# A hybrid decoder layer on one core: keys in natural order in one tile, 144-column scores for the first block, one convolution tap by ScalarE, and a rearranged end

## The chip, the core and the metric

The kernel runs on one core of a Trainium2 chip. Its engines work at the same time, each through a list of instructions of its own: TensorE (PE: matrix products, PEld is its loading of the stationary operand), VectorE (DVE), ScalarE (ACT), GpSimd (POOL) and SyncE (SP, which here only issues transfers). Matrix products land in PSUM banks; everything else lives in SBUF. Transfers go through 16 DMA engines. The metric is the time of one execution on the device, in microseconds (us): the median of several runs.

## The reference, cut to what matters

A sequence of 1,024 rows of 1,024 features gets 16 learned meta rows in front (1,040 positions, all in float32). One layer is computed: a combined input projection feeds an attention group (8 heads of 64 features, 2 key heads, window of 128, one sink per head) and a recurrent group (causal convolution of width 4, gated linear recurrence), then come an output projection and a feed-forward part.

```python
h = concat([meta, x])
u = rmsnorm(h, g_pre_mix)
q, k, v, xr, yr = split(u @ w_in)         # 512, 128, 128, 512, 512 columns
# attention: position i sees keys i-127 .. i, none before the meta rows
s = where(valid, q @ k.T * 64**-0.5, -1e30)
m = max(s.max(-1), sink)
p = exp(s - m) / (exp(s - m).sum(-1) + exp(sink - m))
attn = p @ v
# recurrent group
xr = causal_depthwise_conv(xr, conv_w, conv_b)   # 4 taps and a bias
hr = rg_lru(xr, w_a, b_a, w_x, b_x, lam)
mix = concat([attn, gelu(yr) * hr]) @ w_out
h = h + rmsnorm(mix, g_post_mix)
f = square(relu(rmsnorm(h, g_pre_ffn) @ w_ff1)) @ w_ff2
out = (h + rmsnorm(f, g_post_ffn))[16:]
```

## The kernel before, in words

**Precision.** Every operand of a matrix product is split into a high part in the format fp32r and a low part that holds the rest. ScalarE makes the high part (L96 in `split`, L117 where a scale comes in), VectorE the low part (L99, L118). `mm3` then issues three matmuls (L125 high by high, L128 high by low, L129 low by high) into one PSUM bank. For the scores two matmuls do (L596 with the keys' high part, L600 with the low one): the query tile holds high in 64 of its partitions and low in the other 64, and the key tiles hold the same key twice, once in each half of the partitions. `mirror_k` makes that second copy by transfers that SP issues.

**Stages.** Up to about 58 us the input rows are normalised, transposed and projected to the keys, the values, the first query pair and the first convolution input. From there to about 185 us comes the attention, woven with the remaining projections. Then follow the gates and the recurrence, the output projection (up to about 330 us), and the feed-forward part, which takes two thirds of the time: both its products run as seven block products instead of eight.

**Attention.** The 8 heads are 4 pairs (`j`), the 1,024 positions 8 blocks of 128 in two halves. `scores(j, half, q)` makes the scores of four blocks of a head pair, two blocks to a tile `sn` (tag "c", four slices of 257 columns: 2 heads x 2 blocks). For each block TensorE multiplies the queries with the keys of the block before and of the block itself, 256 columns. Block 0 has only the 16 meta keys before it. In the kernel before these stand in a tile of their own, `km`, at the end of 112 zero columns; its scores come as two groups of 128 columns, 4 matmuls instead of 2, and a second mask (`mask1`) excludes the zero columns. VectorE then adds the mask and takes the row's minimum of the negated scores in one instruction (L616), ScalarE takes the exponential and its sum over 257 columns, the sink being the last (L82). VectorE forms the reciprocal (L628), GpSimd adds the two halves of 128 columns, which hold no common position (L632), VectorE scales by the reciprocal (L633). `attend` runs one step later: TensorE transposes (L644), the result is split (L96, L99), GpSimd separates the two halves again by selects (L648, four for two blocks), TensorE multiplies with the values (L658), and ScalarE and VectorE put the two halves of the product together (L671, L672).

**Fills.** Between these steps `next_fill` puts one projection each: queries of pairs 1 to 3, convolution inputs 1 to 3, the four gates `y`. A query projection ends in L117 (ScalarE) and L118 (VectorE, two of them for each bank), which empty its PSUM bank "acc". A convolution input ends in `sink_x`, a ScalarE copy (L460) in four pieces. Where `y` is given to `new_x`, in this kernel for convolution 2 alone, ScalarE also computes the first tap with the bias from the same bank (L462). `conv` otherwise starts with that tap by VectorE (L682, 1,040 columns), and then adds three taps by VectorE (L687).

**The end.** The last block product is finished by row tile (`finish_late`, tiles `j` = 0 to 3). Tiles 0 to 2 have one part of 512 columns, tile 3 two parts of 256 columns (`HALVES`) in two banks, whose last product's three `q` steps run last. Each part's result is added to the accumulator (first `combine`), ScalarE squares it and sums (L1371), `gffn_b` scales it (second `combine`; both record L1022); then come a square root, its reciprocal (L1416), two output instructions per tile (L1418) and two transfers of 256 KB (L1421). The outputs of a tile are `held`: they may run only behind the next tile's first sum.

**What sets the order.** Each engine's list is made by the scheduler of the framework, which goes by priority (the order in which the code is written, with `deferred` work later), by data, and by the number of buffers of each tag: "b" 17, "c" 8, "d" 4, "e" 2, "ws" 4, "raw" 2, and 2 banks each of "acc", "s", "pt" and "o" in PSUM. Where the code says `behind(name, ins)`, `ins` is to stand behind the instruction `name` of its engine. Tile names in what follows are such a tag and a running number.

## Time and profile before

| | us |
|---|---|
| median of 3 runs | 955.39 (954.9 to 955.9) |
| the profiled execution | 955.25 |
| its span, first instruction to last | 953.5 |
| TensorE busy | 942.0 (99%) |
| VectorE busy | 682.4 (72%) |
| ScalarE busy | 498.3 (52%) |
| GpSimd busy | 152.7 (16%) |
| share of TensorE in the chain that ended last | 88% |

Busy times are those of the profiled execution. In the rows that follow, a row of the chain or of the instructions in order has its start in the span, its duration, the engine, and the operation with what it writes and reads (`out<-in`, numbers left out) or the line. A row of a stretch has the stretch, then the busy time summed over its instructions for TensorE, its weight loads, VectorE, ScalarE and GpSimd, the granted TensorE clock (1.00 is full), the busy share of the DMA engines, and GB/s. A row of a group has the number of its instructions (x), their busy time and the mean duration of one in nanoseconds, or the shortest, the median and the longest.

### The profile page before, as it was taken

To read this page: it belongs to the slowest core of one execution; us is meant where nothing else is said; L and a number is where in the kernel's file an instruction comes from. 1 tells how busy PE (TensorE), PEld (TensorE's weight loads), DVE (VectorE), ACT (ScalarE), POOL (GpSimd) and SP (SyncE) were. 2 spreads that over 40 slices of the span, in tenths; PEclk is the share of its full clock that TensorE was granted. 3 is DMA by queue.
4 is the path that set the end of the run, shared out by engine and by line. 5 is a ranking of instruction groups with operands and counts; after the bars stand their busy time and mean duration, and the time that the engine had idled before them with its cause. 6 is when DMAs were issued, how large, how long until landed. Compare 5 with 4: busy or idle time off the path is not lost.

```text
span 953.5 us, 12448 instructions
## 1 busy us (share of the span) xinstructions
PE 942.0 (99%) x4677; PEld 785.7 (82%) x4677; DVE 682.4 (72%) x968; ACT 498.3 (52%) x822; POOL 152.7 (16%) x196
## 2 busy tenths in 40 slices
...
GB/s 293 49 56 34 45 2 34 67 17 117 42 166 192 153 181 238 158 284 177 218 160 216 157 177 217 226 153 109 171 179 188 208 218 185 185 190 155 116 84 89
DMA packets 85629, 140.76 MB, mean 148 GB/s; under 512 B 5785, under 2 KB 48937, under 8 KB 85569
## 3 DMA queue, kind: packets, MB, share of 16 engines
...
q14 instruction: 24, 0.19, 0.1%
...
## 4 chain that ended last, share of the span: by engine, by line
PE 88%; DVE 7%; ACT 2%; issue 1%; DMA 1%; POOL 1%; DVEq 0%; SPq 0%; ACTq 0%; POOLq 0%
PE ps_acc L125 10%; PE ps_acc L128 10%; PE ps_acc L129 10%; PE ps_pt L128 6%; PE ps_pt L129 6%; PE ps_pt L125 6%; PE ps_s L125 6%; PE ps_s L129 6%; PE ps_s L128 6%; PE ps_o L125 5%; PE ps_o L128 5%; PE ps_o L129 5%; DVE c L852 1%; PE ps_o L658 1%; PE ps_o L996 1%
## 5 line engine op out<-in xcount | busy, mean ns | idle before, releaser
L96 ACT CAST ws<-raw 128x1024 fp32r<-128x1024 f32 (+1 forms) x70 | 71.8, 1025 | 118.9 <-PE ps_o L128 45.8
L99 DVE TENSOR_TENSOR ws<-raw,ws 128x1024 fp32r<-128x1024 f32 (+1 forms) x71 | 85.4, 1203 | 45.5 <-ACT ws L96 45.5
L125 PE MATMUL ps_acc<-a,ws 128*128 128x256 f32 (+2 forms) x256 | 85.5, 334 | 1.1 <-ACT d L460 1.0
L129 PE MATMUL ps_acc<-a,ws 128*128 128x256 f32 (+2 forms) x256 | 85.0, 333 | 0.0
L128 PE MATMUL ps_acc<-a,ws 128*128 128x256 f32 (+2 forms) x256 | 85.0, 332 | 0.0
L99 DVE TENSOR_TENSOR b<-b,b 128x1024 fp32r<-128x1024 f32 (+2 forms) x48 | 57.6, 1199 | 25.5 <-PE ps_o L128 19.8
L96 ACT CAST ws<-e 128x1024 fp32r<-128x1024 f32 x42 | 44.0, 1047 | 57.0 <-PE ps_o L128 31.4
L96 ACT CAST b<-b 128x1024 fp32r<-128x1024 f32 (+2 forms) x48 | 49.5, 1030 | 38.8 <-DVE b L1022 36.4
L99 DVE TENSOR_TENSOR ws<-e,ws 128x1024 fp32r<-128x1024 f32 x42 | 51.3, 1222 | 20.0 <-ACT ws L96 20.0
L648 POOL TENSOR_SCALAR_AFFINE_SELECT c<-c 128x512 fp32r<-128x512 f32 x64 | 55.8, 893 | 26.8 <-ACT c L96 20.6
L125 PEld LDWEIGHTS ps_acc<-a,ws 128*128 128x128 f32 x256 | 48.2, 188 | 6.4 <-ACT d L460 1.2
L129 PEld LDWEIGHTS ps_acc<-a,ws 128*128 128x128 f32 x256 | 48.2, 188 | 5.1 <-issue 0.2
L178 POOL TENSOR_TENSOR rs<-ms,half_pow 128x1 f32<-128x1 f32 x26 | 19.3, 749 | 205.9 <-DVE ms L174 204.7
L128 PEld LDWEIGHTS ps_acc<-a,ws 128*128 128x128 f32 x256 | 48.1, 188 | 4.6 <-issue 0.4
L125 PE MATMUL ps_acc<-ws,b 128*128 128x512 f32 (+1 forms) x120 | 46.3, 385 | 0.0
L129 PE MATMUL ps_acc<-ws,b 128*128 128x512 f32 (+1 forms) x120 | 46.2, 385 | 0.0
L128 PE MATMUL ps_acc<-ws,b 128*128 128x512 f32 (+1 forms) x120 | 46.1, 384 | 0.0
L125 PE MATMUL ps_pt<-ws,b 128*128 128x512 f32 x112 | 44.2, 394 | 0.0
L128 PE MATMUL ps_pt<-ws,b 128*128 128x512 f32 x112 | 44.1, 393 | 0.0
L129 PE MATMUL ps_pt<-ws,b 128*128 128x512 f32 x112 | 43.9, 392 | 0.0
L125 PE MATMUL ps_s<-ws,b 128*128 128x512 f32 x110 | 43.4, 395 | 0.0
L129 PE MATMUL ps_s<-ws,b 128*128 128x512 f32 x110 | 43.2, 393 | 0.0
...
## 6 DMA issues: line engine op xcount, KB each, us to landing
raw<-in_w_ff_dram SPq DMA_DIRECT2D x58, 512.0 KB, 4.4
e<-in_w_ff_dram SPq DMA_DIRECT2D x42, 512.0 KB, 4.1
raw<-in_w_in_dram SPq DMA_DIRECT2D x12, 512.0 KB, 5.1
d<-in_w_ff_dram SPq DMA_DIRECT2D x12, 512.0 KB, 4.2
s_dram<-d POOLq DMA_DIRECT2D x12, 512.0 KB, 4.4
e<-in_w_ff_dram POOLq DMA_DIRECT2D x10, 512.0 KB, 5.8
raw<-in_w_ff_dram POOLq DMA_DIRECT2D x10, 512.0 KB, 5.8
c<-in_x_dram SPq DMA_DIRECT2D x8, 512.0 KB, 8.9
```

What stands on the lines that cost most here:

```text
L96: nc.scalar.copy(hi, src)
L99: low = nc.vector.tensor_tensor(lo, src, f32(hi), op=ALU.subtract).ins
L125: ins = nc.tensor.matmul(dst, lh, rh, start=start, stop=False, skip_group_check=True).ins
L128: nc.tensor.matmul(dst, lh, rl, start=False, stop=False, skip_group_check=True)
L129: last_mm[0] = nc.tensor.matmul(dst, ll, rh, start=False, stop=stop, skip_group_check=True).ins.name
L178: last_pow[0] = nc.gpsimd.tensor_tensor(rs[:n], ms[:n], half_pow[:n], op=ALU.pow).ins.name
L648: nc.gpsimd.affine_select(out=m[:, :, side, :], in_=f32(m)[:, :, 1, :], pattern=[[0, 4], [-sign, P]], compare_op=op, fill=0.0, base=0, cha ...
L658: nc.tensor.matmul(po[:, :, oc : oc + n], v, m[:, :, pc : pc + n], start=first and k == 0, stop=last and k == 1, skip_group_check=True,)
L852: return nc.vector.tensor_tensor_scan(r, a, gi, 0.0, op0=ALU.mult, op1=ALU.add).ins
L996: nc.tensor.transpose(pt[:, i, :], xn[:, kc * P : (kc + 1) * P], ident)
```

## The change

*Keys.* The high and low key tiles (`khh`, `kl`) get 1,040 columns in natural order, the meta keys first. `km` and `mask1` go. Block 0's scores are one group of 144 columns (16 meta keys and 128 of its own), 2 matmuls instead of 4 for each head; L616 and L82 run over 144 and 145 columns there, and GpSimd sets the 112 columns that are now not written to zero, once for each head pair. `sink_k` loses the special case of the meta keys, and the mirror transfers go from 512 to 528 columns for the first half (512 for the second), without the two for `km`.

*Convolution 1.* `new_x` gives `y` for channel group 1 too: its first tap and bias come from ScalarE, in four pieces, and its L682 goes.

*The end.* `finish_late` no longer puts the held outputs of the tile before behind the first sum together. In tile 3, with two parts, one held output is released behind the scaling of each part. Tile 3's own outputs are three, of 512, 256 and 256 columns, issued by SP, ScalarE and SP, instead of two of 512.

The diff, cut:

```diff
@@ -284,13 +284,12 @@
-    khh = [slot("b", [P, T], F32R) for _ in range(2)]
-    kl = [slot("b", [P, T], F32R) for _ in range(2)]
+    khh = [slot("b", [P, TT], F32R) for _ in range(2)]
+    kl = [slot("b", [P, TT], F32R) for _ in range(2)]
     HALF = (slice(0, HD), slice(HD, P))
-    km = const.tile([P, 2, 2, P], F32R, name="km")
     vm = const.tile([P, 2, P], F32R, name="vm")
-    nc.gpsimd.memset(f32(km), 0.0)
-    idle, still = bank("acc"), km.rearrange("p a b c -> p (a b c)")
+    nc.gpsimd.memset(f32(khh[0][:, :512]), 0.0)
+    idle, still = bank("acc"), khh[0]
@@ -409,24 +408,12 @@
-    def put_k(hh, lo, src):
+    def sink_k(acc, t0, n):
+        c = slice(t0, t0 + n)
         for h in range(2):
...
-            nc.scalar.copy(hh[h][r], src[r])
-            nc.vector.tensor_tensor(lo[h][r], src[r], f32(hh[h][r]), op=ALU.subtract)
-
-    def sink_k(acc, t0, n):
-        o = 0
-        if t0 == 0:
-            put_k(
-                [km[:, h, 0, META] for h in range(2)],
-                [km[:, h, 1, META] for h in range(2)], acc[:, 0:NMETA],
-            )
-            o = NMETA
-        c = slice(t0 + o - NMETA, t0 - NMETA + n)
-        put_k(
-            [khh[0][:, c], khh[1][:, c]], [kl[0][:, c], kl[1][:, c]], acc[:, o:]
-        )
+            nc.scalar.copy(khh[h][r, c], acc[r])
+            nc.vector.tensor_tensor(kl[h][r, c], acc[r], f32(khh[h][r, c]), op=ALU.subtract)
@@ -454,7 +441,7 @@
 
     def new_x(tag="d", c=0):
         xr = slot(tag, [P, TT])
-        y = slot("d", [P, TT]) if c == 2 else None
+        y = slot("d", [P, TT]) if c == 1 or c == 2 else None
 
         def sink_x(acc, t0, n):
             nc.scalar.copy(xr[:, t0 : t0 + n], acc)
@@ -496,12 +483,9 @@
         if b == 1:
-            for h in range(2):
-                r, o = HALF[h], HALF[1 - h]
-                nc.sync.dma_start(f32(km[o, h]), f32(km[r, h]))
-            mirror_k(slice(0, 512))
+            mirror_k(slice(0, 528))
         elif b == 3:
-            mirror_k(slice(512, T))
+            mirror_k(slice(528, TT))
@@ -524,9 +508,6 @@
-    mask1 = const.tile([P, 256], F32, name="mask1")
-    nc.gpsimd.memset(mask1[:, 0 : P - NMETA], NEG)
-    nc.gpsimd.tensor_copy(mask1[:, P - NMETA :], mask[:, P - NMETA :])
@@ -576,6 +557,8 @@
+    KEYS, KEYS_0 = (0, 256), (P - NMETA, 256)
+
     def scores(j, half, q):
 
@@ -588,41 +571,34 @@
+            spans = [KEYS if 4 * half + 2 * bp + i else KEYS_0 for i in range(2)]
+            if spans[0] is KEYS_0:
+                nc.gpsimd.memset(
+                    sn.rearrange("p (h i) k -> p h i k", h=2)[:, :, 0, 0 : P - NMETA], 0.0
+                )
             for h in range(2):
                 sp_ = bank("s", (P, 2, 256))
-
-                def qk(dst, b, hi, lo):
+                for i, (w0, w1) in enumerate(spans):
+                    b = 4 * half + 2 * bp + i
                     c = slice(b * P, (b + 1) * P)
...
-                for i in range(2):
-                    b = 4 * half + 2 * bp + i
-                    if b == 0:
-                        qk(sp_[:, i, 0:P], b, km[:, g, 0, :], km[:, g, 1, :])
-                        qk(sp_[:, i, P:256], b, khh[g][:, 0:P], kl[g][:, 0:P])
-                    else:
-                        c = slice((b - 1) * P, (b + 1) * P)
-                        qk(sp_[:, i, :], b, khh[g][:, c], kl[g][:, c])
-                for i in range(2):
-                    b = 4 * half + 2 * bp + i
+                    o = NMETA + (b - 1) * P
+                    for n, k_ in enumerate((khh, kl)):
+                        nc.tensor.matmul(
+                            sp_[:, i, w0:w1], q[h][:, c], k_[g][:, o + w0 : o + w1],
+                            start=n == 0, stop=n == 1, skip_group_check=True,
+                        )
+                for i, (w0, w1) in enumerate(spans):
                     k = 2 * h + i
                     top = nc.vector.tensor_tensor_reduce(
-                        out=sn[:, k, 0:256], in0=sp_[:, i, :],
-                        in1=mask1 if b == 0 else mask, scale=-1.0,
+                        out=sn[:, k, w0:w1], in0=sp_[:, i, w0:w1],
+                        in1=mask[:, w0:w1], scale=-1.0,
                         scalar=nsink[:, 2 * j + h : 2 * j + h + 1],
                         op0=ALU.add, op1=ALU.min, accum_out=negm[:, k : k + 1],
                     ).ins
                     if (j, half, bp, k) == (3, 0, 0, 3):
                         behind(top.name, *held_back)
                     lut(
-                        sn[:, k, :], sn[:, k, :], AF.Exp, scale=-1.0,
+                        sn[:, k, w0:], sn[:, k, w0:], AF.Exp, scale=-1.0,
                         bias=negm[:, k : k + 1], accum_out=den[:, k : k + 1],
                     )
             nc.vector.reciprocal(rden, den)
@@ -1404,17 +1380,21 @@
         for k, c in enumerate(parts):
             yield k
             last = combine(acc[:, c], y[k], acc[:, c], ALU.add).name
-            behind(last, *held)
-            held.clear()
             part = squares(y[k], acc[:, c], k)
-            combine(o[:, c], acc[:, c], gffn_b[:, c], ALU.mult)
+            scaled = combine(o[:, c], acc[:, c], gffn_b[:, c], ALU.mult)
+            if len(parts) == 1:
+                behind(last, *held)
+                held.clear()
+            else:
+                behind(scaled.name, held.pop(0))
             if k < len(parts) - 1:
                 nc.vector.tensor_tensor(ssq, ssq, part, op=ALU.add)
...
-        for c, eng in zip(COLS[::-1], (nc.sync, nc.scalar)):
+        cols = COLS[1:] + (HALVES if j == 3 else COLS[:1])
+        for c, eng in zip(cols, (nc.sync, nc.scalar, nc.sync)):
             held.append(nc.vector.scalar_tensor_tensor(
                 o[:, c], o[:, c], rs, h[:, c], op0=ALU.mult, op1=ALU.add
             ).ins)
```

In what follows, the rows of the changed kernel carry its own line numbers: L592 is the L616 of before, L604 L628, L609 L633, L647 and L648 are L671 and L672, L663 is L687, L447 L460, L998 L1022, L1391 L1412, L1395 L1416, L1398 L1418. L82, L96, L99, L117 and L118 are unchanged.

**VectorE around the query projection of pair 2.** Before, the second bank (ps_acc_1415) is emptied by the two L118. The ps_o are banks of the products with the values, c tiles are scores, e_1444 collects the output of head pair 0's second half.

```order
L99 TENSOR_TENSOR ws_1550<-raw_1547,ws_1549 128x1024
L118 SCALAR_TENSOR_TENSOR b_1384<-ps_acc_1415,b_1384 64x512
L672 TENSOR_TENSOR e_1444<-ps_o_1482,e_1444 64x256
L616 ISA c_1721,negm<-ps_s_1726,mask_906,nsink 128x256
L616 ISA negm 128x1
L616 ISA c_1721,negm<-ps_s_1726,mask,nsink 128x256
L616 ISA negm 128x1
L672 TENSOR_TENSOR e_1666<-ps_o_1680,e_1666 64x256
L628 RECIPROCAL rden<-den 128x4
L99 TENSOR_TENSOR c_1845<-ps_pt_1846,c_1844 128x4x128
L118 SCALAR_TENSOR_TENSOR b_1385<-ps_acc_1415,b_1385 64x512
L672 TENSOR_TENSOR e_1444<-ps_o_1482,e_1444 64x256
```

After, the second bank is ps_acc_1402, and e_1431 is that output. Two pieces of VectorE's list, with five rows between them:

```order
L663 SCALAR_TENSOR_TENSOR d_1149<-d_1148,prm,d_1149 128x1037
L648 TENSOR_TENSOR e_1431<-ps_o_1469,e_1431 64x256
L118 SCALAR_TENSOR_TENSOR b_1372<-ps_acc_1373,b_1372 64x512
L648 TENSOR_TENSOR e_1431<-ps_o_1469,e_1431 64x256
L99 TENSOR_TENSOR b_970<-e_1431,b_969 128x512
```

```order
L118 SCALAR_TENSOR_TENSOR b_1371<-ps_acc_1402,b_1371 64x512
L648 TENSOR_TENSOR e_1653<-ps_o_1667,e_1653 64x256
L592 ISA c_1708,negm<-ps_s_1714,mask,nsink 128x144
L592 ISA negm 128x1
L592 ISA c_1708,negm<-ps_s_1714,mask,nsink 128x256
L592 ISA negm 128x1
L604 RECIPROCAL rden<-den 128x4
L648 TENSOR_TENSOR e_1653<-ps_o_1691,e_1653 64x256
L99 TENSOR_TENSOR c_1829<-ps_pt_1830,c_1828 128x4x128
L118 SCALAR_TENSOR_TENSOR b_1372<-ps_acc_1402,b_1372 64x512
```

Behind the first L118 of the second bank stood one L672 of that first output (ps_o_1482), and another one behind the second L118; now both (ps_o_1469) stand ahead of both L118, with the low part of that output's split (b_970). Of the next output (ps_o_1680 before, ps_o_1667 and ps_o_1691 after) two sums instead of one stand ahead of the second L118. No L682 of convolution 1 is left ahead.

**VectorE and ScalarE around the query projection of pair 3 and the copy of convolution input 3.** VectorE before (c_2151 are scores of head pair 2, ws_1949 the low part of a weight, ps_acc_1814 the query bank):

```order
L616 ISA c_2121,negm<-ps_s_2137,mask,nsink 128x256
L616 ISA negm 128x1
L99 TENSOR_TENSOR ws_1949<-raw_1946,ws_1948 128x1024
L616 ISA c_2151,negm<-ps_s_2156,mask,nsink 128x256
L616 ISA negm 128x1
L616 ISA c_2151,negm<-ps_s_2156,mask,nsink 128x256
L616 ISA negm 128x1
L118 SCALAR_TENSOR_TENSOR b_1783<-ps_acc_1814,b_1783 64x512
L672 TENSOR_TENSOR e_2236<-ps_o_2250,e_2236 64x256
```

VectorE after:

```order
L592 ISA c_2105,negm<-ps_s_2120,mask,nsink 128x256
L592 ISA negm 128x1
L592 ISA c_2132,negm<-ps_s_2137,mask,nsink 128x256
L592 ISA negm 128x1
L592 ISA c_2132,negm<-ps_s_2137,mask,nsink 128x256
L592 ISA negm 128x1
L99 TENSOR_TENSOR ws_1933<-raw_1930,ws_1932 128x1024
L118 SCALAR_TENSOR_TENSOR b_1767<-ps_acc_1798,b_1767 64x512
L648 TENSOR_TENSOR e_2217<-ps_o_2231,e_2217 64x256
```

The low part of the weight (L99) stood ahead of the two L616 of the second c tile, and stands behind them now. ScalarE before, at the same place (d_1952 takes the convolution input):

```order
L117 ACTIVATE b_1784<-ps_acc_1814 64x512
L671 COPY e_2236<-ps_o_2250 64x256
L671 COPY e_2236<-ps_o_2274 64x256
L460 COPY d_1952<-ps_acc_1953 128x272
L82 ACTIVATE c_2151,den<-c_2151,negm 128x257 x2
L82 ACTIVATE c_2287,den<-c_2287,negm 128x257 x2
```

ScalarE after:

```order
L117 ACTIVATE b_1768<-ps_acc_1798 64x512
L647 COPY e_2217<-ps_o_2231 64x256
L647 COPY e_2217<-ps_o_2255 64x256
L82 ACTIVATE c_2132,den<-c_2132,negm 128x257
L447 COPY d_1936<-ps_acc_1937 128x272
L82 ACTIVATE c_2132,den<-c_2132,negm 128x257
L82 ACTIVATE c_2268,den<-c_2268,negm 128x257 x2
```

The copy that empties the convolution's bank (L460, now L447) has one more exponential (L82) of the second c tile ahead of it.

**VectorE at the end.** Before (a_7937 are the outputs of tile 2, a_7986 those of tile 3, ps_o_7744 and ps_acc_7747 the two banks of tile 3's two parts):

```order
L1416 RECIPROCAL rs<-root 128x1
L1022 TENSOR_TENSOR a_6940<-ps_o_7744,a_6940 128x256
L1418 SCALAR_TENSOR_TENSOR a_7937<-a_7937,rs,d_7935 128x512 x2
L1022 TENSOR_TENSOR a_7986<-a_6940,a_7436 128x256
L1412 TENSOR_TENSOR late_7987<-late_7987,sq_8122 128x1
L1022 TENSOR_TENSOR a_6940<-ps_acc_7747,a_6940 128x256
L1022 TENSOR_TENSOR a_7986<-a_6940,a_7436 128x256
L1416 RECIPROCAL rs<-root 128x1
L1418 SCALAR_TENSOR_TENSOR a_7986<-a_7986,rs,d_7984 128x512 x2
```

After (a_7918 and a_7967 are these outputs, ps_o_7725 and ps_acc_7728 the banks):

```order
L1395 RECIPROCAL rs<-root 128x1
L998 TENSOR_TENSOR a_6921<-ps_o_7725,a_6921 128x256
L998 TENSOR_TENSOR a_7967<-a_6921,a_7417 128x256
L1398 SCALAR_TENSOR_TENSOR a_7918<-a_7918,rs,d_7916 128x512
L1391 TENSOR_TENSOR late_7968<-late_7968,sq_8103 128x1
L998 TENSOR_TENSOR a_6921<-ps_acc_7728,a_6921 128x256
L998 TENSOR_TENSOR a_7967<-a_6921,a_7417 128x256
L1398 SCALAR_TENSOR_TENSOR a_7918<-a_7918,rs,d_7916 128x512
L1395 RECIPROCAL rs<-root 128x1
L1398 SCALAR_TENSOR_TENSOR a_7967<-a_7967,rs,d_7965 128x512
L1398 SCALAR_TENSOR_TENSOR a_7967<-a_7967,rs,d_7965 128x256 x2
```

Both outputs of tile 2 stood behind the first sum of tile 3. Now one stands behind the first part's scaling and the other behind the second part's. The outputs of tile 3 are three rows' worth of instructions instead of two. On TensorE the list is the same, but for numbers, from about 149 us of the profile before to the end.

8 lines of the change are left out of this document (removed).

## The prediction

> **What bounds the kernel now.** I read the page first, then busy time in stretches of ten microseconds, then the chain of work that ended last where a stretch shows TensorE idle, and last the instructions in order of time at the scores and at the end.
>
> ```profile
> span 953.5 us, 12448 instructions
> PE 942.0 (99%) x4677; PEld 785.7 (82%) x4677; DVE 682.4 (72%) x968; ACT 498.3 (52%) x822; POOL 152.7 (16%) x196
> PE 88%; DVE 7%; ACT 2%; issue 1%; DMA 1%; POOL 1%; DVEq 0%; SPq 0%; ACTq 0%; POOLq 0%
> ```
>
> TensorE is busy 942.0 of 953.5 us and carries 88% of the chain. So a microsecond of matrix work taken out is worth a microsecond, if nothing else ends last just behind it. The average hides that, the stretches tell it (after the sum: PE, PEld, DVE, ACT, POOL):
>
> ```profile
> 80.00:90.00 10.00, 9.86 (x82) 9.61 (x81) 9.46 (x28) 7.11 (x19) 5.78 (x9) 1.00 0.19 56
> 150.00:160.00 10.00, 9.05 (x71) 8.66 (x70) 9.77 (x26) 6.24 (x20) 3.76 (x3) 1.00 0.25 67
> 180.00:190.00 10.00, 9.09 (x44) 7.32 (x43) 8.25 (x13) 5.29 (x9) 3.42 (x4) 1.00 0.17 52
> ```
>
> In the attention stage VectorE is as full as TensorE (9.46 and 9.77 of 10), and TensorE idles 0.14 + 0.95 + 0.91 = 2.0 us in these three stretches. All the clocks are 1.00, so the clock plays no part.
>
> **The change part by part.**
>
> *Scores of block 0.* One head of head pair 2, before:
>
> ```profile
> 117.07 0.22 PE L596 MATMUL ps_s<-km,b 128*128 128x128 f32 x1
> 117.13 0.27 PE L600 MATMUL ps_s<-km,b 128*128 128x128 f32 x1
> 117.24 0.28 PE L596 MATMUL ps_s<-b,b 128*128 128x128 f32 x1
> 117.35 0.28 PE L600 MATMUL ps_s<-b,b 128*128 128x128 f32 x1
> 117.46 0.33 PE L596 MATMUL ps_s<-b,b 128*128 128x256 f32 x1
> 117.63 0.28 PE L600 MATMUL ps_s<-b,b 128*128 128x256 f32 x1
> 117.75 0.29 PE L129 MATMUL ps_acc<-a,ws 128*128 128x272 f32 x1
> ```
>
> Start to start, six matmuls take 0.68 us. A 128-column one takes 0.11, a 256-column one 0.12 to 0.17. The new 144 columns lie between: two at 0.11 to 0.12, and block 1's two at 0.23 to 0.29, so 0.45 to 0.53. That saves 0.15 to 0.23 per head, and I take 0.20. Eight heads: 1.6 us (1.2 to 1.8). The Trainium skill, TensorE: Matmul & The Clock Gate, section Back-to-back issue gap, has about 81 ns for a sustained 128-column matmul; the trace's 0.11 us is slower and decides. By the page the sixteen fewer matmuls would be an estimated 1.3 us.
>
> What arrives is another matter. Pairs 0 and 1 (four heads, 0.8 us) lie ahead of this piece of the chain:
>
> ```profile
> 78.80 0.50 ACT c L82 x2
> 79.37 1.48 POOL c L632
> ...
> 86.33 0.65 POOL c L648
> 87.02 0.50 PE ps_o L658
> ```
>
> At 87.02 TensorE waits for a GpSimd select, behind eight microseconds of ScalarE, GpSimd and VectorE. That chain doesn't get shorter by a faster TensorE. It starts earlier only by what pair 0's shorter reductions and exponentials give:
>
> ```profile
> L616 DVE CUSTOM_DVE_ANT_0 c<-ps_s,mask,nsink 128x256 f32<-128x256 f32 x64 | 28.2, 477 | 0.9 <-PE ps_s L600 0.4
> L672 DVE TENSOR_TENSOR e<-ps_o,e 64x256 f32<-64x256 f32 x32 | 13.1, 418 | 0.7
> L682 DVE TENSOR_SCALAR d<-d,prm x1: 1128/1128/1128, 105.9 to 105.9; 128x1040 f32<-128x1040 f32 x1
> L462 ACT ACTIVATE d<-ps_acc,prm x4: 559/576/584, 119.8 to 144.8; 128x256 f32<-128x256 f32 x3, 128x272 f32<-128x272 f32 x1
> ```
>
> A reduction of 256 columns takes 0.477 us. With 144 it saves between nothing and 112/256 of it (0.21); I take 0.12, as some of it is fixed. Two of them in pair 0 give 0.2 us. **Term 1: 0.2** (0 to 0.8). Pair 2 (0.4 us) lies between 87 and 140, where the chain is matmul upon matmul. **Term 2: 0.4** (0 to 0.5). Pair 3's 0.4 falls into the wait at 156 and counts nothing by itself.
>
> *First tap of convolution 1.* VectorE loses one instruction of 1.13 us at 105.9, ScalarE gains four of 0.56 to 0.58. TensorE waits for neither there, so I cost both at 0. The cover is ScalarE's idle time (7.11 of 10 busy at 80 to 90). Were it gone, the four copies would free a PSUM bank up to 4 x 0.58 = 2.3 us late in all, and TensorE, which refills that bank, would wait.
>
> *Moved order, second query bank.* VectorE's second half of the pair-2 query (L118) frees a PSUM bank; two waits of the new order press on it:
>
> ```profile
> 118.88 0.69 DVE L118 SCALAR_TENSOR_TENSOR b<-ps_acc,b 64x512 fp32r<-64x512 f32 x1
> ...
> 137.58 1.21 DVE L99 TENSOR_TENSOR b<-e,b 128x512 fp32r<-128x512 f32 x1 [0.69 <-ACT b L96]
> ```
> ```profile
> 119.84 0.28 PE L125 MATMUL ps_acc<-a,ws 128*128 128x256 f32 x1
> ```
>
> It ends at 119.57, and TensorE takes the bank at 119.84: 0.27 us of reserve. Ahead of it now stand two more L672 (0.42 each) and a low part of L99 with its hand-off from ScalarE (about 1.2, and 0.69 of waiting), 2.7 in all. Gone are L682 (1.13) and 0.12 of a reduction, and by term 1 all comes 0.2 earlier: 1.3 late. Against that TensorE itself comes later, since six probability matmuls stand ahead of the bank now, and VectorE waits in that stretch already; I take 0 (0 to 1.3 lost), nearer to the row's reserve.
>
> *Keys in one tile.* Four small ScalarE and VectorE pieces, two SP transfers (the mirrored meta keys) and a mask go, four GpSimd memsets come (5.78 of 10 busy there, each well ahead of its reader). Mirrors grow from 512 to 528 columns and are issued where they were, behind projections; SP's later loads move up by two places. All at 0; a late mirror would hold the first scores one for one.
>
> *The wait at 156.*
>
> ```profile
> 153.01 1.14 DVE ws L99
> ...
> 156.98 0.40 ACT d L460
> ...
> 157.41 0.39 PE ps_acc L125
> ```
>
> TensorE waits here for ScalarE's copy (L460), which stands behind VectorE's reductions. Two of these now run ahead of the 1.14 us of L99, one pair is shorter (0.2), but the copy stands behind one more exponential, which itself needs a later reduction. Gain at most 1.14 + 0.2, loss about 0.5 for the exponential: **Term 3: 0.6** (-0.5 to 0.95, the stretch's idle time).
>
> *The wait at 184.*
>
> ```profile
> 179.76 0.43 DVE e L672
> ...
> 180.22 0.70 DVE c L99
> ...
> 184.35 0.74 PE ps_o L658 x3
> ```
>
> The split that GpSimd's selects wait for (L99 at 180.22) changes places with L672: 0.43 earlier. The selects behind it stay three in a row. **Term 4: 0.3** (0 to 0.43).
>
> *The end.*
>
> ```profile
> 946.81 0.28 PE L129 MATMUL ps_acc<-a,b 128*128 128x256 f32 x1
> ```
> ```profile
> 945.84 1.40 DVE L1418 SCALAR_TENSOR_TENSOR a<-a,rs,d 128x512 f32<-128x512 f32 x2
> 947.16 0.41 DVE L1022 TENSOR_TENSOR a<-a,a 128x256 f32<-128x256 f32 x1
> ...
> 947.56 0.41 DVE L1022 TENSOR_TENSOR a<-ps_acc,a 128x256 f32<-128x256 f32 x1
> 948.01 0.42 DVE L1022 TENSOR_TENSOR a<-a,a 128x256 f32<-128x256 f32 x1
> 948.88 0.16 DVE L1416 RECIPROCAL rs<-root 128x1 f32<-128x1 f32 x1 [0.45 <-ACT root L82]
> 949.08 1.41 DVE L1418 SCALAR_TENSOR_TENSOR a<-a,rs,d 128x512 f32<-128x512 f32 x2
> ```
>
> The last matmul ends at 947.09, its sum starts at 947.56: VectorE is late, as both outputs of row tile 2 stand ahead. One of them now moves behind, so the sum can start 0.45 sooner. That output (0.70) then stands ahead of the reciprocal: sum 947.13, product 947.58, output 947.98 to 948.6, reciprocal 948.6 instead of 948.88. Three outputs of 0.70, 0.41 and 0.41 less their overlap take about what two took, so the last ends 0.3 earlier. Its transfer is half as large:
>
> ```profile
> out_dram<-raw SPq DMA_DIRECT2D x8, 512.0 KB, 2.9
> b<-b SPq DMA_DIRECT2D x8, 128.0 KB, 2.2
> out_dram<-a ACTq DMA_DIRECT2D x4, 256.0 KB, 2.1
> ```
>
> 512 KB land in 2.9 and 256 in 2.1, so on that line 128 KB land in 1.7; by the 128 KB row (2.2, another kind) nothing is gained. I take 0.3 (0 to 0.4). **Term 5: 0.6** (0.2 to 0.8). The Trainium skill speaks against this part: DMA: Bandwidth & Descriptors, section Anatomy of one DMA, puts about 2.0 us of a transfer down as fixed. By that floor the half transfer gains 0.1 instead of 0.3, and the sum is 0.2 smaller; the 2.1 agrees with such a floor, and no row of a small write to DRAM is here to decide.
>
> **The sum.** 0.2 + 0.4 + 0.6 + 0.3 + 0.6 = 2.1 us. The profiled execution took 955.25 (1.75 around its span) and would take 953.15. The median of the runs, 955.39, is 0.14 above it: 953.3.
>
> **The rivals.**
>
> *The gain is swallowed in attention.* VectorE is the bound there, and terms 3 and 4 rest on its order alone. For it speaks 9.46 to 9.77 of 10 busy, against it that 1.13 us leave that very engine. Then terms 1 and 5 stay, and little more: 0.9, so 954.5.
>
> *The waits go.* With VectorE 1.13 + 8 x 0.12 us lighter, the three idle stretches close, and the 1.6 of matrix work comes through whole. That would be 1.6 + 2.0 + 0.6 = 4.2 at the most; with most of it, 951.5. Against it: the waits at 87 and 184 end on GpSimd, which the change relieves little.
>
> *Slower: the second query bank.* If the new order's hand-offs between VectorE and ScalarE cost 0.69 each at six places ahead of L118 (4.1), and one ScalarE tap (0.58) falls among them, L118 comes 4.7 late. Less some 0.6 of reserve (0.27 and what TensorE is later by) TensorE loses 4.1 once, and all behind it shifts: 955.39 - 2.1 + 4.1 = 957.4. It decides from 2.7 us of lateness. For it speaks the small reserve, and that the new order is read from lists without times; against it that VectorE has one long instruction less just ahead.
>
> **How the numbers follow.** Within 0.2% (1.91 us, about what a measurement of this kernel can tell from no change) lie 953.48 to 957.30. My forecast, 953.3 with its own range 952.4 to 954.3, gets 0.46, of it 0.32 below 953.48. Swallowed gets 0.19, waits gone 0.13, slower 0.22, of it 0.16 above 957.30. So faster 0.45, same 0.39, slower 0.16. The range, 951.4 to 957.4, leaves out half of slower (0.11) and the lower part of waits gone (0.06).
>
> **What would show it.** Right: sixteen fewer score matmuls; TensorE's wait at 87 longer (about 0.9) and not shorter; the matmul behind the copy L460 at about 156.2; the wait at 184 shorter; the last sum 0.05 behind the last matmul, and the span ending 0.6 sooner after it. Wrong: a new wait of TensorE between 95 and 140, above all at the second query bank; a wait at 156 that grew; a last transfer that lands 2.1 after its issue.

## The result, and the profile after

The changed kernel takes 957.32 us (median of 19 runs, 955.24 to 959.77), the kernel before beside it 955.90 (19 runs, 954.90 to 957.64). The ratio is 1.0015, with a 95% interval of 1.0009 to 1.0021: slower by 1.4 us, where 2.1 us faster was forecast. It lies inside the 0.2% called "same", but clear of no change, and a second session gave 1.0018 (1.0010 to 1.0027). The profiled execution took 957.16, of it 955.1 span; that is 1.91 more than the profiled execution before.

Its page, the rows that answer to those of before:

```profile
span 955.1 us, 12416 instructions
PE 941.6 (99%) x4661; PEld 784.8 (82%) x4661; DVE 681.3 (71%) x966; ACT 498.4 (52%) x824; POOL 150.4 (16%) x198
PE 84%; DVE 9%; ACT 2%; POOL 2%; issue 2%; DMA 1%; DVEq 0%; SPq 0%; POOLq 0%; ACTq 0%
```

TensorE has sixteen matmuls and 0.4 us less to do and yet a longer span; its share of the chain fell from 88% to 84%. So there is more waiting. The best way to see where is the start of the same matmul in both traces, place by place:

| at (us, before) | place | changed kernel later by |
|---|---|---|
| 58.0 | ahead of the first scores | 0.22 |
| 85.8 | ahead of the wait at 87 | -0.50 |
| 87.1 | behind it | 0.00 |
| 126.0 | behind the second query bank | 0.79 |
| 157.5 | behind the wait for the copy L460 | 0.94 |
| 184.5 | behind the wait for the selects | -0.05 |
| 192 | gates begin | -0.09 |
| 690 | feed-forward, second product | 0.02 |
| 699 | nine microseconds on | 0.98 |
| 946.8 | last matmul | 1.25 |

The attention, from 58 to 192, gains 0.31, where 1.5 was forecast. The rest is lost where I had looked for nothing: 0.96 at 698 us, 0.38 in small pieces (0.11 up to 690, 0.27 behind 699), 0.31 at the end (6.77 us from the last matmul to the end of the span, 6.46 before) and 0.31 outside the span (2.06 us for 1.75). With the 0.22 from before the attention that is 1.87 of the 1.91.

The stretches tell the same of the attention (the last two rows answer to 0.95 and 0.91 of idle time before):

```profile
80.00:90.00 10.00, 9.36 (x76) 8.98 (x75) 9.49 (x30) 7.62 (x22) 6.07 (x10) 1.00 0.20 56
120.00:130.00 10.00, 9.08 (x75) 8.78 (x74) 9.40 (x30) 8.01 (x26) 6.16 (x8) 1.00 0.10 31
150.00:160.00 10.00, 8.57 (x66) 8.12 (x65) 9.76 (x24) 6.64 (x20) 3.09 (x2) 1.00 0.27 74
180.00:190.00 10.00, 10.00 (x49) 8.31 (x48) 8.64 (x14) 4.92 (x9) 2.74 (x3) 1.00 0.17 53
```

In the first three VectorE is about as full as it was (9.4 to 9.8 of 10). Of TensorE's waits the one at 184 is gone, and the ones at 87 and 156 grew. In 120 to 130, where TensorE was busy for all of the 10.00 us before, it now idles 0.92. Below, a wait is the time from the start of the last matmul ahead of it, less that matmul's own 0.11 to 0.23.

VectorE and TensorE at the second query bank, instructions in order:

```profile
114.98 0.69 DVE L99 TENSOR_TENSOR b<-e,b 128x512 fp32r<-128x512 f32 x1 [0.69 <-ACT b L96]
117.77 0.68 DVE L118 SCALAR_TENSOR_TENSOR b<-ps_acc,b 64x512 fp32r<-64x512 f32 x1
120.62 0.69 DVE L118 SCALAR_TENSOR_TENSOR b<-ps_acc,b 64x512 fp32r<-64x512 f32 x1
```
```profile
121.45 0.36 PE L125 MATMUL ps_acc<-a,ws 128*128 128x256 f32 x1 [0.92 <-DVE b L118]
```

The last L118 starts at 120.62, 1.74 later than before, with the split and its 0.69 us of waiting for ScalarE ahead of it. TensorE stands for 1.1 us.

The wait for ScalarE's copy, now L447, by the chain:

```profile
154.27 1.14 DVE ws L99
155.41 0.03 issue
155.44 0.70 DVE b L118
156.14 0.02 issue
156.16 0.60 ACT b L117
...
156.78 0.63 ACT e L647 x2
...
157.44 0.60 ACT c L82 x2
158.04 0.28 ACT d L447
158.31 0.04 issue
158.36 0.39 PE ps_acc L125
```

The copy starts at 157.94 instead of 156.98 and the wait is 1.6 instead of 1.1. The chain shows both reasons: L118 starts 0.45 later than before (155.44 for 154.99, still behind the weight's low part L99), and 0.5 us of exponentials (L82) stand ahead of the copy.

The wait that is new at 698 us lies in the second product of the feed-forward part. Its chain:

```profile
688.31 6.93 DMA raw<-in_w_ff_dram
695.46 1.02 issue
696.48 0.62 DVE b L998
697.09 0.52 issue
697.61 1.23 DVE ws L99
698.88 0.50 PE ps_acc L128
```

A weight load of 512 KB, issued at 688.31, comes 7 us later. VectorE adds it to another one (L998) at 695.33, splits it (L99), and TensorE gets it 0.9 us late. Before, the same load was issued at 688.59, and the addition ran at 692.68:

```profile
692.68 1.23 DVE L1022 TENSOR_TENSOR e<-e,raw 128x1024 f32<-128x1024 f32 x1 [2.91 <-DMA raw<-in_w_ff_dram]
```

The end, VectorE:

```profile
948.38 0.42 DVE L998 TENSOR_TENSOR a<-ps_acc,a 128x256 f32<-128x256 f32 x1
948.84 0.42 DVE L998 TENSOR_TENSOR a<-a,a 128x256 f32<-128x256 f32 x1
949.18 0.74 DVE L1398 SCALAR_TENSOR_TENSOR a<-a,rs,d 128x512 f32<-128x512 f32 x1
949.84 0.15 DVE L1395 RECIPROCAL rs<-root 128x1 f32<-128x1 f32 x1
950.13 1.54 DVE L1398 SCALAR_TENSOR_TENSOR a<-a,rs,d 128x512 f32<-128x512 f32 x3
```

The last matmul ends at 948.34 and its sum starts 0.04 behind it, as forecast. The outputs end 3.34 behind that matmul (3.41 before). The loss comes in the transfer, whose landing the view of the transfers has:

```profile
out_dram<-a SPq DMA_DIRECT2D x1, 128.0 KB, 2.4
```

128 KB land in 2.4 us, where 256 KB took 2.1.

### The profile page after: what moved, and what is told of

It reads as the page before. It is cut to its first block, busy times and chain, and to the rows that moved or that the text cites. A ratio compares the mean times of both kernels' runs of the same rounds, so it can differ in the third digit from the quotient of the medians.

```text
span 955.1 us, 12416 instructions
## 1 busy us (share of the span) xinstructions
PE 941.6 (99%) x4661; PEld 784.8 (82%) x4661; DVE 681.3 (71%) x966; ACT 498.4 (52%) x824; POOL 150.4 (16%) x198
## 3 DMA queue, kind: packets, MB, share of 16 engines
q10 hardware_dynamic: 864, 1.97, 0.6%
## 4 chain that ended last, share of the span: by engine, by line
PE 84%; DVE 9%; ACT 2%; POOL 2%; issue 2%; DMA 1%; DVEq 0%; SPq 0%; POOLq 0%; ACTq 0%
PE ps_acc L125 9%; PE ps_acc L128 9%; PE ps_acc L129 9%; PE ps_pt L128 6%; PE ps_pt L129 6%; PE ps_pt L125 6%; PE ps_s L129 6%; PE ps_s L128 6%; PE ps_s L125 6%; PE ps_o L125 5%; PE ps_o L128 5%; PE ps_o L129 5%; POOL c L624 1%; DVE ws L99 1%; DVE c L828 1%
## 5 line engine op out<-in xcount | busy, mean ns | idle before, releaser
L96 ACT CAST ws<-raw 128x1024 fp32r<-128x1024 f32 (+1 forms) x70 | 71.7, 1024 | 117.8 <-PE ps_o L128 46.9
L99 DVE TENSOR_TENSOR ws<-raw,ws 128x1024 fp32r<-128x1024 f32 (+1 forms) x71 | 85.5, 1204 | 45.4 <-ACT ws L96 45.4
L99 DVE TENSOR_TENSOR b<-b,b 128x1024 fp32r<-128x1024 f32 (+2 forms) x48 | 57.6, 1199 | 24.1 <-PE ps_o L128 15.9
L96 ACT CAST ws<-e 128x1024 fp32r<-128x1024 f32 x42 | 44.0, 1047 | 56.7 <-PE ps_o L128 31.7
L96 ACT CAST b<-b 128x1024 fp32r<-128x1024 f32 (+2 forms) x48 | 49.4, 1030 | 39.7 <-DVE b L998 37.0
L99 DVE TENSOR_TENSOR ws<-e,ws 128x1024 fp32r<-128x1024 f32 x42 | 51.3, 1222 | 22.7 <-ACT ws L96 22.7
L624 POOL TENSOR_SCALAR_AFFINE_SELECT c<-c 128x512 fp32r<-128x512 f32 x64 | 51.8, 831 | 25.5 <-ACT c L96 19.3
```

What stands on the lines that cost most here:

```text
L96: nc.scalar.copy(hi, src)
L99: low = nc.vector.tensor_tensor(lo, src, f32(hi), op=ALU.subtract).ins
L624: nc.gpsimd.affine_select(out=m[:, :, side, :], in_=f32(m)[:, :, 1, :], pattern=[[0, 4], [-sign, P]], compare_op=op, fill=0.0, base=0, cha ...
```

## The experiments

Each kernel was timed beside the kernel before on the same chip; a ratio is to that. Three (e7, e8 and e13) ran once, for the trace alone: 957.52, 957.66 and 956.86 us. What is said of stretches, waits and transfers is read from one trace of each kernel.

### One part at a time

**The end alone**: the kernel before with the new `finish_late`.

> Only the rearranged end, attention as before. Theory A (the end costs, because the last transfer stands among four others that are still landing): the last output instruction ends 3.3 us after the last matmul as in the changed kernel (3.4 before), its transfer lands 2.4 us after its issue (2.1 before), the span ends 6.75 us behind the last matmul (6.46 before), so the median is 0.3 us above before, 0.2 to 0.4. Rival (the step of my prediction): 0.3 to 0.6 us faster. The order of all engines up to the end is that of before, so waits in the feed-forward part should come as rarely as before; if they come more often without any change ahead of them, the spread will show it.

Median 956.02 against 956.20, ratio 0.9999 (0.9990 to 1.0008). In the trace the outputs end 3.23 behind the last matmul (3.41 before), the span 6.90 behind it (6.46 before). The loss of 0.44 is in the trace alone: the interval reaches from 1.0 gained to 0.8 lost, so it can't tell this from nothing, nor does it exclude the gain of 0.6.

**Keys and tap alone**: the changed kernel with the old `finish_late`.

> Keys and tap as in the changed kernel, the end as before. Theory A (attention is even: the 1.6 us of matmuls saved and the wait at 184 that went are eaten by the waits at 87, 121 and 157; the rest of the loss of 1.4 us is a late weight load at about 698 us that comes in some executions): the query bank's wait at 121 us is there with 1.1 us, TensorE at 185 us is within 0.3 us of before, and the time is before plus 0 where no load is late, plus 0.9 to 1.2 where one is; median 0 to 1.2 above before. Theory B (attention is what costs): TensorE is 1 us or more behind before at 185 us in this trace. If the loads' waits are chance alone and not tied to this part, the median is within 0.3 us of before.

Median 958.06 against 956.20, ratio 1.0024 (1.0013 to 1.0035). From 58 to 192 us TensorE gains 0.25, with waits of 1.1 at 121 and 1.6 at 157. At 698 it waits for 1.0 again. So attention is even or a little better, and the wait at 698 comes with the keys and the tap, not with the end.

One more loss comes with them. The end of this kernel is that of before, and yet its outputs end 3.61 behind the last matmul (3.41 before) and its span 6.78 (6.46). Between the last reciprocal and the outputs VectorE stands for 0.27, where it stood for 0.04. The first output in e10, a kernel further down with the same attention and end:

```profile
949.30 0.75 DVE L1394 SCALAR_TENSOR_TENSOR a<-a,rs,d 128x512 f32<-128x512 f32 x1 [0.27 <-DVE rs L1392]
```

The gap is there in five of the six traces with keys, tap and the old end (e2, e10 to e13, not e14), and in no trace with keys or tap alone. Why it comes isn't shown. In these five the span ends 6.66 to 6.78 behind the last matmul; with the new end, in five traces of the changed kernel and its variants (e5, e16 to e18), 6.75 to 6.96. The middle values are 6.77 and 6.79: with keys and tap in place the new end neither saves nor costs anything that these traces show, and the 0.31 that the changed kernel loses at its end can't be put down to the new end alone.

**Keys alone, and the tap alone:**

```diff
 # keys alone: changed kernel, old finish_late, and
-        y = slot("d", [P, TT]) if c == 1 or c == 2 else None
+        y = slot("d", [P, TT]) if c == 2 else None
 # tap alone: kernel before, and
-        y = slot("d", [P, TT]) if c == 2 else None
+        y = slot("d", [P, TT]) if c == 1 or c == 2 else None
```

> Only the keys in one tile and the 144-column scores; first tap of convolution 1 by VectorE again, the end as before. Theory (the order around the second query bank comes from the tap's leaving VectorE, since the sums and the split of the output before moved up into its place): no wait of TensorE at 121 us above 0.3 us, TensorE at 185 us 0.5 to 1.5 us ahead of before, so 0.5 to 1.5 us faster where no load is late. Rival (the order changed by the shorter scores): the wait at 121 is there with about 1 us, and the time is before plus or minus 0.3.

> Only the first tap of convolution 1 by ScalarE; keys, masks and end as before. Theory (the tap moves the order at the second query bank): a wait at the second query bank of about 1 us, TensorE at 185 us 0.3 to 1.2 us behind before. Rival (VectorE is relieved by 1.1 us and nothing else): no such wait, TensorE at 185 us level or up to 1 us ahead.

Keys alone: 960.41 against 956.20, ratio 1.0044 (1.0032 to 1.0057). From 58 to 220 us TensorE loses 1.9; the largest wait is 1.8 at 126, behind a tap of VectorE (L663, 1.84 us) and ScalarE's L449. At 698 there is a wait of 0.5, and behind it TensorE loses another 1.9, 1.0 of it in one wait at 763. Tap alone: 955.90, ratio 0.9997 (0.9988 to 1.0006), TensorE 0.23 ahead from 58 to 192, no wait at 121 and none at 698. Both theories that I had written for these two fall: the tap does not cost, and the keys without the tap cost most. Of the two rivals, that of the tap came true. With the tap alone the split also stands ahead of the L118 (114.73), and that L118 ends at 120.58; but TensorE, with the longer scores of before, comes to the bank only at 121.31. In the changed kernel the four score matmuls ahead of the bank start at 119.90 and lie 0.12 apart, so there TensorE would have been at the bank at about 120.4. So the wait at 121 takes both: the order, and a TensorE that the shorter scores bring there earlier.

### The end: order or pieces

```diff
 # order alone: kernel before, new finish_late, but
-        cols = COLS[1:] + (HALVES if j == 3 else COLS[:1])
+        cols = COLS[::-1]
 # pieces alone: kernel before, old order, but
-        for c, eng in zip(COLS[::-1], (nc.sync, nc.scalar)):
+        cols = COLS[1:] + (HALVES if j == 3 else COLS[:1])
+        for c, eng in zip(cols, (nc.sync, nc.scalar, nc.sync)):
```

> The kernel before, with only the order at the end changed: the held outputs of tile 2 behind the scaling of the two parts, tile 3's outputs in two pieces of 512 columns as before. By its trace: the first sum starts 0.05 behind the last matmul (as with all of the new end), the last output ends 3.2 to 3.4 us behind it; if the late landing (2.4 to 2.7 us instead of 2.1) comes from the late held output's transfer in flight, the last transfer lands 2.3 or more after its issue, and the span ends 6.6 to 6.9 behind the last matmul; if it comes from the pieces, it lands in 2.1 and the span ends 6.2 to 6.4 behind it (6.46 before).

> The kernel before, with only tile 3's outputs in 512, 256 and 256 columns; the held outputs both behind the first sum as before. By its trace: last output 3.4 us behind the last matmul (3.41 before). If the pieces cost, because the last transfer of 128 KB stands behind two others that were issued within 0.8 us, it lands 2.3 or more after its issue and the span ends 6.7 to 6.9 behind the last matmul; if smaller is faster (the step of my prediction), it lands in 1.7 to 2.0, and the span ends 6.1 to 6.4 behind it.

Transfers with the order alone, then with the pieces alone:

```profile
out_dram<-a SPq DMA_DIRECT2D x4, 256.0 KB, 2.6
out_dram<-a ACTq DMA_DIRECT2D x4, 256.0 KB, 2.8
```
```profile
out_dram<-a ACTq DMA_DIRECT2D x1, 128.0 KB, 2.1
out_dram<-a SPq DMA_DIRECT2D x1, 128.0 KB, 2.1
```

With the order alone, the outputs end earlier (3.10 behind the last matmul, 3.41 before) and the span later (6.94 behind it, 6.46 before): what VectorE gains is given back by the transfers. A row is the median of those landings that the trace has; taken singly, the last transfer of SP landed 3.2 after its issue and the last of ScalarE 2.8 (2.0 and 2.1 before), and the 2.6 has one of 2.1 of an earlier tile in it. With the pieces alone, 128 KB land in 2.1, as 256 KB did, and the span ends 6.59 behind the last matmul (6.61 in e19, a kernel below with the end of before). So in these traces the order is what costs: the second held output of tile 2 is issued 1.6 us behind the last matmul (0.2 before). The last transfers are issued 0.9 and 1.5 behind it, when it must still be under way, as no output here lands in under 1.9. The pieces neither gain nor cost. (The wait of 0.7 at 698 that showed in the trace with the pieces comes back below.)

### The wait at 698 us

The trace holds each packet of a transfer. A 16 KB packet on the instruction queue comes every 29 us or so, in step with TensorE's list; in the changed kernel one starts at 692.67 and takes 0.93 us. By 693.8 all but ten of the late load's some 270 packets have landed; these ten come behind the fetch, and VectorE can add the load 1.1 to 1.6 us later against TensorE than in kernels whose fetch lies elsewhere (e10, e5). Before, the same fetch came at 687.56, 10.2 us instead of 5.1 ahead of the matmul that precedes the wait. VectorE's addition, which then ran 5.1 ahead of that matmul, runs 2.5 ahead of it in the changed kernel, and 3.6 and 4.1 ahead in e10 and e5. Over all traces of this study it runs 3.3 to 5.1 ahead in the thirteen without a wait there, and 2.1 to 2.8 in the seven with one. The sixteen matmuls that are gone are 32 instructions with their weight loads, and I take it that they shift every later fetch. Idle matmuls at the start shift it back:

```diff
 # changed kernel (or the variant named), and
-    idling(11)
+    idling(27, 208)      # e5 and e10; e16: 19, 296; e17: 31, 182
 # kernel before, and
-    idling(11)
+    idling(123, 46)      # e9: fetches as in the changed kernel
```

> The changed kernel, and the 11 idle matmuls of 512 columns at its start made 27 of 208, so that TensorE's list of instructions is as long again as before at every place from the attention on, with the same idle work. Theory (in the changed kernel a 16 KB fetch of TensorE's own instructions, which comes about every 29 us, has moved from 687.6 to 692.7 us because 32 instructions are gone ahead of it; there it stands in front of the last packets of the weight load that VectorE and then TensorE wait for): the fetch is back at about 687.6, TensorE's wait of 0.9 at 698 us is gone, the attention is unchanged (1.1 at 121, 1.6 at 157), the median is 0.8 to 1.2 below that of the changed kernel, so within 0.6 of before. Rival (the load is late because the loop of loads runs 1.7 us earlier there, or by the tiles' other addresses): the wait at 698 stays at 0.8 to 1.0, and so does the time of the changed kernel.

> The kernel before, with its 11 idle matmuls of 512 columns at the start made 123 of 46, so that TensorE's list is 224 instructions longer there and its 16 KB instruction fetches (every 256 instructions) come where those of the changed kernel come; the attention, the feed-forward part and the end are those of before. Theory (the fetch in front of the load's last packets makes the wait at 698): a fetch starts about 5 us ahead of the last matmul before the wait (10 us in the kernel before), the load lands 1 to 1.6 later against TensorE's place than without it, and TensorE waits 0.5 to 1.2 there where the load came behind the GpSimd transfer, nothing where it came ahead of it. Median 0.3 to 0.9 above before, if the start loses nothing. Rival (the wait comes by the loads' order alone, and belongs to the changed keys by another way): no wait there, median within 0.3 of before, apart from what the start itself loses.

> Keys and tap as in the changed kernel, the end as before, and 27 idle matmuls of 208 columns at the start, so that the fetches come where those of before come: the changed kernel without the two losses that the runs point to (the end 0.3, the fetch 0.9). Theory (the attention itself gains 0.3 from its first score to the gates, and nothing else differs): no wait at 698 from a fetch, span behind the last matmul 6.4 to 6.6, median 0 to 0.5 below before. Against the attention part with the end as before and its own fetches (958.06, 0.24% above before) that is 1 to 2 us less. Rival (the tiles' other addresses or the two transfers fewer cost something in the feed-forward part that no fetch explains): 0.5 to 1.5 above before.

> The changed kernel with 19 idle matmuls of 296 columns for the 11 of 512: TensorE's instruction fetch comes half as far from where the changed kernel has it, at about 7.5 us ahead of the matmul at 698 instead of 5.1. Theory (the wait there needs the fetch to meet the last packets of the load, which run about 6 to 4 us ahead): no wait at 698 in the trace, the load combined 3.3 us or more ahead; median span 0.3 to 1.0 below the changed kernel's in the same session. Rival (it is there by the loads' order, and the runs without it were chance): wait of 0.5 to 1.2 as in the changed kernel, span the same.

> The changed kernel with 31 idle matmuls of 182 columns: the fetch comes about 11 us ahead of the matmul at 698, while no load is due. Same expectations: by the theory no wait, median span 0.3 to 1.0 below the changed kernel's; by the rival the wait and the span of the changed kernel.

> The changed kernel itself, for the same session as the two other phases and for a second trace. Theory: the wait at 698 is there again with 0.5 to 1.2 us, the fetch about 5 us ahead of it, the end 6.8 to 7.0 behind the last matmul, time outside the span 2.05. Rival (the wait of the first trace was chance): no wait at 698 in this trace.

VectorE's addition of the late load: the changed kernel again, then with the fetch moved back (e5), then the kernel before with the fetch moved to where the changed kernel has it (e9, whose start lost 24.9 us):

```profile
694.91 1.23 DVE L998 TENSOR_TENSOR e<-e,raw 128x1024 f32<-128x1024 f32 x1 [5.98 <-DMA raw<-in_w_ff_dram]
```
```profile
693.91 1.23 DVE L998 TENSOR_TENSOR e<-e,raw 128x1024 f32<-128x1024 f32 x1 [4.32 <-DMA raw<-in_w_ff_dram]
```
```profile
721.48 1.23 DVE L1022 TENSOR_TENSOR e<-e,raw 128x1024 f32<-128x1024 f32 x1 [6.18 <-DMA raw<-in_w_ff_dram]
```
```profile
725.03 0.50 PE L128 MATMUL ps_acc<-ws,b 128*128 128x512 f32 x1 [0.95 <-DVE ws L99]
```

| kernel | fetch ahead of the matmul | wait at 698 | ratio |
|---|---|---|---|
| changed, first and second trace | 5.1, 5.1 | 0.9, 0.9 | 1.0015, 1.0018 |
| e9, before with their fetches | 5.0 | 1.1 | 1.0281 (start) |
| e5, e16, e17, changed with others | 10.0, 9.9, 10.5 | 0 | 1.0014, 1.0012, 1.0041 (e17's start lost 3.7) |
| e2, changed, old end | 5.1 | 1.0 | 1.0024 |
| e10, the same with other fetches | 9.8 | 0 | 1.0011 (1.0002 to 1.0020) |

In all the traces of this study, the wait was there in each of the six with the fetch 4.6 to 5.4 us ahead (0.5 to 1.2 us; keys alone, and a kernel below, among them), and in one of fourteen with the fetch 9.5 to 10.9 ahead: the one with the pieces alone, where the load shared its time with GpSimd's instead of following it. That the fetch makes the wait in these executions is shown, by e9 in a kernel that is otherwise that of before.

How much of the median it is, isn't. With the old end, moving the fetch took the span's median from 956.0 to 955.2 (e2, e10, in different sessions; the intervals of their ratios overlap). With the new end it did nothing that can be seen: 955.35 in the changed kernel (30 runs in two sessions), 955.3 in e5 and e16 (23 runs). The 19 runs of the changed kernel spread over 4.5 us, so a difference of 0.9 needs many. e16 also moved the fetch further than I had worked out: it gives back 16 of the 32 instructions, and the fetch went all the way (to 9.9, not 7.5). So its place doesn't follow the number of instructions one for one.

e10 still lies 0.9 us over before, where it was expected 0 to 0.5 below. About 0.3 of this lie outside the span (at the end of this section), and 0.31 in its trace at the end, 6.77 behind the last matmul instead of the 6.4 to 6.6 that were expected, by the gap ahead of the outputs. At the last matmul its trace is level with before (0.02 later). Two other causes were tried, the tiles' addresses (3 KB less of constants) and the two transfers fewer:

```diff
 # e10, and in the places of km and mask1 (memsets left out)
+    pad = const.tile([P, 2, 2, P], F32, name="pad")
+    pad1 = const.tile([P, 256], F32, name="pad1")
 # e12 also, ahead of mirror_k(slice(0, 528))
+                nc.sync.dma_start(pad[o, h], pad[r, h])
```

> As the attention part with the end of before and the fetches where before has them, and 3 KB of every partition are taken up again where the key and mask tiles of before lay, so that all later tiles lie where they lay in before. What is open is why that attention part, whose trace stands level with before at the last matmul (0.02) and whose profiled execution took 956.05, has a median of 957.21, 0.9 above before. If the tiles' addresses cost it (rival): the median falls to 955.9 to 956.5, before plus or minus 0.3. If not: 956.8 to 957.6, as without the 3 KB.

> The same with the 3 KB, and two small transfers by SP where before mirrors its meta keys, so that every later transfer has the place in SP's list, and the semaphore, that it had in before. If the number of transfers ahead decides over the later loads (rival): median 955.9 to 956.5, while the one without these two stays at 956.8 to 957.6. If neither addresses nor transfers matter (theory: the loads' phase in the feed-forward part is thrown from execution to execution, and the changed attention starts it from another one): both medians at 956.8 to 957.6, with executions from 956 to 959.

Both 956.95 against 955.83: ratios 1.0016 (1.0007 to 1.0025) and 1.0011 (1.0003 to 1.0020). Both lie where e10 lies, so neither is the cause, though a part smaller than these intervals isn't excluded.

### The waits of the attention

**At 121**, the split and its hand-off behind the second bank:

```diff
 # cut: in attend, for head pair 0's second half, the split is written out as high and low
+            behind(query[0][0].name, high)   # L117, last of the bank
+            behind(query[0][1].name, low)    # L118
```

> The changed kernel, and the split of head pair 0's second half (b from e; ScalarE's high part and VectorE's low part with its wait of 0.69 us for it) is put behind the two L118 of the second query bank. Theory (this split with its hand-off is what made those L118 1.7 us late, and their lateness is TensorE's wait of 1.1 at 121 us): the wait at 121 falls to 0 to 0.3, TensorE is 0.8 to 1.1 earlier at 125 us than in the changed kernel. Theory A on what is left of it at the end: VectorE is the bound of the stretch, so the work only moves and TensorE's waits at 157 and 184 take it back, the time is that of the changed kernel within 0.4. Rival B: the gain comes through, 0.7 to 1.1 below the changed kernel.

The last L118 now starts at 119.30 instead of 120.62, and the wait at 121 is gone; at 149 us TensorE is 1.7 ahead of the changed kernel. But the scheduler rearranges what follows. The weight's low part (L99) now starts just behind GpSimd's addition and takes 2.34 us instead of 1.22, TensorE waits for 2.3 at 154, and then its granted clock falls to 0.50 from 158.3 to 161.7 (one stretch of it):

```profile
159.00:160.00 1.00, 1.00 (x7) 1.00 (x7) 1.00 (x4) 0.82 (x4) 0.10 (x1) 0.50 0.08 16
```

There sixteen matmuls of 256 columns take 0.21 each from start to start instead of 0.12, 1.4 us more. The kernel is slower still: 959.66 against 956.14, ratio 1.0031 (1.0019 to 1.0043). Both expectations for the time missed, that of the changed kernel within 0.4 and 0.7 to 1.1 less: the gain came at 121 and was lost again from 154 on.

**At 157**, on the kernel of e10: the copy ahead of the exponential (e13), and the weight's low part behind the L118 (e14).

```diff
 # both cut: lines that only keep names are left out
 # e13, behind the lut(...) of scores
+                    if (j, half, bp, k) == (3, 0, 1, 2):
+                        behind(first_x[0], power)      # copy L460 of convolution 3
 # e14, where held_back is put behind a reduction
+                        behind(query[-2][1].name, *held_back)   # L118 of the bank
```

> Keys and tap as in the changed kernel, end and fetches as before, and ScalarE's copy that empties the convolution's bank put ahead of the one exponential that the new order had placed before it. Theory (of the 0.96 us by which that copy starts later than before, 0.50 is this exponential and 0.46 is VectorE's L118, which stands behind all four reductions and the weight's low part, as in before): the copy starts 0.4 to 0.5 earlier against the score matmuls ahead of it, TensorE's wait falls from 1.6 to 1.1, and TensorE at 165 us is 0.4 to 0.5 ahead of the kernel without this. At 192 us 0 to 0.5 of it is left. Rival (the copy waits for VectorE alone): wait stays at 1.5 to 1.6.

> Keys and tap as in the changed kernel, end and fetches as before, and the weight's low part (L99, 1.14 us) on VectorE put behind the L118 that ScalarE's L117 and then the copy wait for; by the scheduler's new list the copy also stands ahead of the exponential. Theory (the step of my prediction for the wait at 156 had the wrong place: the gain of 1.14 needs the low part behind that L118, and moving it behind two reductions alone gives nothing): the wait falls from 1.6 to 0 to 0.3, TensorE is 1.2 to 1.6 ahead at 165 us of the kernel without this. If it comes through to the end, the median is 955.4 to 956.0, level with before or up to 0.5 below; rival (VectorE is the bound, the low part then comes too late for the next projection): a new wait of 0.7 or more between 158 and 185, and a median of 956.6 to 957.6.

TensorE behind the wait at 157 in e10, in e13, and e13 again at 185:

```profile
158.55 0.38 PE L125 MATMUL ps_acc<-a,ws 128*128 128x256 f32 x1 [1.43 <-ACT d L447]
```
```profile
158.00 0.39 PE L125 MATMUL ps_acc<-a,ws 128*128 128x256 f32 x1 [0.95 <-ACT d L449]
```
```profile
185.23 0.50 PE L125 MATMUL ps_acc<-a,ws 128*128 128x512 f32 x1 [0.29 <-DVE d L697]
```

The exponential is 0.5 of the wait, as worked out. TensorE at 157 is 0.54 ahead of e10, and at 192 it is 0.11 behind: a wait at 185 for VectorE, which e10 doesn't have, takes it back. In e14 the L118 does come earlier, but the low part then starts behind GpSimd's addition and takes 1.94 us instead of 1.22, what stands behind it is late, and the wait is 2.0 instead of 1.6. And behind it TensorE runs slower (stretches of e14; clock, share and GB/s are the last three):

```profile
157.00:159.00 2.00, 0.22 (x2) 0.03 (x2) 1.94 (x6) 1.11 (x3) 0.00 (x0) 1.00 0.05 11
160.00:161.00 1.00, 1.00 (x7) 1.00 (x7) 0.97 (x3) 0.52 (x3) 0.40 (x1) 0.50 0.83 239
161.00:162.00 1.00, 1.00 (x6) 1.00 (x6) 0.97 (x4) 0.18 (x1) 0.89 (x1) 0.50 0.00 0
164.00:166.00 2.00, 2.00 (x19) 2.00 (x18) 1.43 (x5) 1.18 (x5) 0.50 (x1) 1.00 0.00 0
```

The granted clock falls to 0.50 for about 3.4 us, and a 256-column matmul takes 0.21 from start to start instead of 0.12; TensorE loses another 1.5 (1.60 later than before at 157.4, 3.10 at 165). Median 957.96 against 956.48, ratio 1.0019 (1.0007 to 1.0031). So neither move gives anything that lasts to the gates. e13 came as expected up to 165 us and left nothing at 192, because TensorE then waits for VectorE. In e14 neither expectation came, since the wait itself grew.

### Outside the span

The prediction took the 1.75 us around the span as given. The runs have 1.65 to 1.84 in each of 136 runs of before, and 1.98 to 2.12 in each of the changed kernel's first 19. Over all the kernels the median was 1.66 to 1.82 where the trace has up to 1,078 ScalarE instructions, 2.02 to 2.16 where it has 1,079 or more; before has 1,075, the changed kernel 1,079. (These counts have the instructions that only wait or issue in them; the page's 822 and 824 leave them out.) So four copies of one column were added to before:

```diff
     lut(root, half_pow, AF.Sqrt, scale=-1.0)
+    more = const.tile([P, 4], F32, name="more")
+    for i in range(4):
+        nc.scalar.copy(more[:, i : i + 1], half_pow)
```

> The kernel before with four more ScalarE copies of one column near its start, where ScalarE waits; nothing else. Theory (the time outside the span steps with the length of ScalarE's list: it was 1.7 us in all kernels with up to 1,078 ScalarE instructions in their trace and 2.04 in all with 1,079 and more, of which the changed kernel is one; before has 1,075): 1,079 instructions, and 2.0 to 2.1 us outside the span instead of 1.71, in every execution; the span itself as before, 954.4 plus or minus 0.6. Rival (the step belongs to the taps by ScalarE or to their place): 1.7 outside the span.

1,079 instructions, and 1.97 to 2.08 outside the span in 9 of 9 runs, with 1.65 to 1.82 in the 11 of before beside them. Four instructions of next to no work cost 0.34 us outside the span. Why the step stands there isn't shown. It also hides something: the tap alone has 1,079, and is level in its time with a span 0.65 shorter than before beside it (medians 953.8 and 954.45).

## Why the prediction was wrong

*Scores.* The sizes were right: one head of pair 0 saves 0.24 (0.20 forecast), a reduction of 144 columns takes 0.36 instead of 0.48. From 58 to 85.8 us TensorE gains 0.72, the wait at 87 grows from 0.3 to 0.8 and takes 0.5 of it, and 0.22 is left. That is term 1, 0.2; it is 0.20 to 0.22 in the other traces of this attention too (e2, e5, e10, e18).

*Tap.* Costed at 0, and the tap alone is level in its time, outside the span included.

*Second query bank.* Here the first step failed: "I take 0 (0 to 1.3 lost), nearer to the row's reserve". The order showed two more sums, a split and a hand-off ahead, and I worked out 1.3 us late; it was 1.74. I then set it against a TensorE that would come later, and gave that no size. It did come later, but by only 0.54: the first of the four score matmuls ahead of the bank starts at 119.90 instead of 119.37. With the 0.27 of reserve that covers 0.8. So by the prediction's own 1.3 the term was 0.5 and not 0, and by the measured 1.74 it is 0.9. In e4, with the long scores, TensorE is 1.5 later than before (0.35 of it from the start) and doesn't wait. The wait is 1.1, near the end of my range, and it ate term 2. The slower rival named the place, and overdrew its price (4.1). That its time, 957.4, is so near the measured 957.3 is luck: most of the measured loss lies elsewhere.

*Wait at 156.* The second step that failed: "Gain at most 1.14". The copy waits for L117, this for L118, and L118 stands behind the low part and all four reductions in both orders; to change their places ahead of it gives nothing. The loss of 0.5 for the exponential came as said. Term 3 was 0.6 of gain and is 0.5 of loss. e14 shows that moving the low part itself behind that L118 doesn't give the 1.14 either.

*Wait at 184.* Forecast 0.3 shorter, and it went whole, 1.1. TensorE came later by then, and the three selects took 2.81 in all instead of 3.26. So the attention's four terms, 1.5 together, are 0.31, and 0.09 behind the wait at 87: the rival "swallowed in attention" was right, by the mechanism that e13 shows. What one wait gives, the next takes, while VectorE is full.

*The end.* Here the third step failed. VectorE's part of term 5 is about right with the order alone (0.31 earlier), 0.18 with all of the new end (e1), where a third output stands ahead, and 0.07 in the changed kernel, where 0.14 and not 0.04 stand between the reciprocal and the outputs. The transfer's part, 0.3, has the wrong sign: I read its landing from rows of transfers that stand alone, and the new order puts it beside others. Half the size gave nothing even with the old order (2.1, e8). But the old end would have saved nothing here: with the new keys and the tap it loses 0.31 too (e2, e10), by a gap on VectorE that the prediction didn't have.

*The frame of the sum.* Nothing behind the attention was in it. Loads and fetches were taken as they were in the trace of before, and so was the time around the span. The one costs 0.96 in the trace, the other 0.31 to 0.34.

The three terms with places, 0.31 gained, and 0.31 and 0.34 lost, make 0.3 of loss of the median's 1.4. The rest, about 1, is left for the feed-forward part. The late load accounts for most of it in the traces, but its share of the median stays open, as do about 0.27 us that every kernel with the new keys loses in small pieces between 699 and 900 (keys alone more).
